# Fetching the cached rows of the sample stream one step early, into the buffers of the sample tokens

## The chip, the cores and the metric

The kernel runs on one core of one Trainium2 chip. The metric is the device time of one execution in microseconds (us); the number quoted for a kernel is the median of its timed runs.

## The reference, cut to what matters

The reference is one step of a one-layer encoder: a SwiGLU feed-forward block, an input projection with two groups of attention heads, and a second SwiGLU block. There are 1024 prompt tokens and 64 sample tokens; the sample tokens also attend to 1024 cached rows of keys and values.

```python
def macaron_half(x, g, b, w_gate, w_up, w_down):
    return layer_norm(ALPHA * x + 0.5 * swiglu(x, w_gate, w_up, w_down), g, b)

def mixer_sample(q_a, ..., pos, c_k_a, c_v_a, c_kidx, c_k_b, c_v_b, c_logf):
    ka_all = jnp.concatenate([c_k_a, k_a], axis=1)
    va_all = jnp.concatenate([c_v_a, v_a], axis=1)
    kb_all = jnp.concatenate([c_k_b, k_b], axis=1)
    vb_all = jnp.concatenate([c_v_b, v_b], axis=1)
    cum = jnp.cumsum(jnp.concatenate([c_logf, logf_b], axis=1), axis=1)
    ...
```

The cached rows are inputs: they depend on nothing that the kernel computes. The kernel needs them in another form, keys transposed, and every value split into a high and a low part (two float32r numbers whose sum is the float32 number). It makes that form while the first feed-forward block runs, and stores it in DRAM for the attention, which comes some hundreds of us later.

## The kernel before, in words

**The stage.** `ffn_a` (L203) computes gate and up products of a feed-forward block. It runs twice: L862 for the first block, with the cached work (`cgen`) as its argument `during`, and L1980 for the second, with an empty iterator. Otherwise both calls do the same work. It steps over j = 0 to 10, two slices of the hidden width each: `body0` (L258) for j = 0, and `body(j, u)` (L314) for j from 1, first for the gate weights (u = 0), then for the up weights (u = 1). Products follow a fast matrix-multiplication scheme with seven products of half-size blocks, each made of 12 matmuls (three for the split parts, by four).

**One body.** `raw_of` (L408, its DMA is L415) fetches two raw weight tiles of 128x1024, each by two DMAs. `split` (L107) copies a tile to its high part on ACT (L108) and makes the low part on DVE (L109). Four sums S1 to S4 of raw blocks are made on POOL (L327), then split on ACT (L330) and DVE (L331) to `Sh` and `Sl`. The products then go to PSUM and are evicted into a ring of 12 SBUF tiles (`ringz`): L340 on ACT, L342, L353, L355, L359, L361 on DVE, the gate's activation at L253 on ACT, gate times up at L256 on DVE. After u = 1, `emit_h` (L228) makes three sums on POOL (L231 to L234) and stores seven tiles (L236, to `hd0A` and `hd0S`). L353 of the next j writes a ring tile that one of these stores must have left. `emit_w` (L238) fetches two tiles of the down weights (L242), makes four sums (L245 to L248) and stores them (L250).

**The sample tokens.** The 64 sample rows ride along as matmuls `fs`. `sample(j)` (L372) evicts them to `sv` (L374, L375), makes `ssg` (L253, L256), and after the next body (`flush_late`, L390) transposes it on PE (L382) and stores it as `hs` (L384, L385).

**The buffers.** A tile is asked for by a tag; all tiles of a tag share so many buffers, and a DMA into a tile waits until an earlier tile of that tag is read for the last time. The tags that matter: `st` (3 buffers of 128x1024): the raw weights, and the cached rows `ckv` and `cka`; `wh` and `wl` (3 each): the split weights, and the split cached rows `chl`, `cha` and `cvt`; `hsh` (2 of 128x512): `ssg`, and the forget values `cf`; `hsl` (2 of 128x384): `hs`, and `lt`, `cm` of `cum_chunk`; `ssum` (4): `sv` and S1 to S4.

**The cached work.** `cached_all` (L841) is a generator; `ffn_a` calls `next(during)` four times per j (L311 in `body0`, L343 and L356 in `body`). Of each of the eight blocks of 128 cached rows (`cached_block`, L798) the first call fetches keys and values of group B into one `st` tile (L801, L802), transposes the keys by four PE transposes (L805, into the PSUM tile `ckb`), splits them to `chl` and stores both parts (L809); the second splits the values to `cvt` and stores them (L815); the third fetches group A's keys and values into another `st` tile (L818, L819), transposes (L821, into `cka`), splits to `cha`, and stores (L825, L828). Four last calls handle the forget values: a memset on POOL (L847), a fetch (L848), two transposes (L852, into `lfc`), a running sum on DVE (L836 to L838) and a store (L839). That is 28 calls, so it lasts to the end of j = 6.

**The order of the work.** All DMAs are issued from one queue, SP's. A scheduler orders each engine's instructions ahead of time, by their place in the program and by when it reckons that their inputs and buffers are there; on the chip each engine works through its list in order, and an instruction that waits holds up all behind it.

Of the kernel before, what the change touches and what calls it, by code (L numbers as in the profile page):

```python
# [9 lines left out]
F32 = mybir.dt.float32  # L10
F32R = mybir.dt.float32r
# [8 lines left out]
P = 128  # L20
# [9 lines left out]
HD = 64  # L30
# [17 lines left out]
def hybrid_step(ctx: ExitStack, tc: tile.TileContext, i, o):  # L48
    nc = tc.nc
    V, S, G, PE, DMA = nc.vector, nc.scalar, nc.gpsimd, nc.tensor, nc.sync  # L50
# [3 lines left out]
    ck_a = i["cache_k_a"].rearrange("l b s h d -> (l b s) h d")  # L54
    cv_a = i["cache_v_a"].rearrange("l b s h d -> (l b s) h d")
    ck_i = i["cache_kidx_a"].rearrange("l b s d -> (l b s) d")
    ck_b = i["cache_k_b"].rearrange("l b s h d -> (l b s) h d")
    cv_b = i["cache_v_b"].rearrange("l b s h d -> (l b s) h d")
    clf = i["cache_logf_b"].rearrange("l b s h -> (l b s) h")
# [9 lines left out]
    mp = ctx.enter_context(tc.tile_pool(name="mp", bufs=2, side="right"))  # L69
    sp = ctx.enter_context(tc.tile_pool(name="sp", bufs=4, side="right"))  # L70
    wp = ctx.enter_context(tc.tile_pool(name="wp", bufs=3, side="right"))
# [6 lines left out]
    def sm(name):  # L78
        return ps.tile([P, 512], F32, tag="sm", name=name, bufs=4)
# [7 lines left out]
    ident = cst.tile([P, P], F32, name="ident")  # L87
# [16 lines left out]
    def f(ap):  # L104
        return ap.bitcast(F32)

    def split(hi, lo, src):  # L107
        S.copy(hi, src)  # L108
        V.tensor_tensor(lo, src, f(hi), ALU.subtract)  # L109
# [645 lines left out]
    def load_x(xo, wg, wu):  # L755
# [12 lines left out]
        def put(t, hf):  # L768
# [11 lines left out]
    kacT = dp.tile([1, 2, P, PAST], F32, name="kacT")  # L780
    kbcT = dp.tile([4, 2, P, PAST], F32, name="kbcT")
    vaS, vbS, vacS, vbcS = (dp.tile([nh, P, 8, 2, HD], F32, name=nm)
                            for nm, nh in (("vaS", 2), ("vbS", 8), ("vacS", 2), ("vbcS", 8)))
    vaN, vbN = (dp.tile([DEC, nh, 2, HD], F32, name=nm) for nm, nh in (("vaN", 2), ("vbN", 8)))

    def v_rows(d, dn, t, h0, nh):
        return dn[:, h0:h0 + nh] if t == 8 else d[h0:h0 + nh, :, t].rearrange("h p s d -> p h s d")
    cumd_p = dp.tile([8, SEQ], F32, name="cumd_p")
    cumd_s = dp.tile([8, TT], F32, name="cumd_s")
# [5 lines left out]

    last_c = cst.tile([32, 1], F32, name="last_c")

    def cached_block(a):  # L798
        rs_ = slice(a * P, (a + 1) * P)
        kv = wp.tile([P, 1024], F32, tag="st", name="ckv")  # L800
        DMA.dma_start(kv[:, 0:512].rearrange("p (h d) -> p h d", h=8), ck_b[rs_])  # L801
        DMA.dma_start(kv[:, 512:1024].rearrange("p (h d) -> p h d", h=8), cv_b[rs_])  # L802
        pt = sm(f"ckb{a}")
        for q in range(4):
            PE.transpose(pt[:, q * P:(q + 1) * P], kv[:, q * P:(q + 1) * P], ident)  # L805
        hl = wp.tile([P, 1024], F32R, tag="wh", name="chl")
        split(hl[:, 0:512], hl[:, 512:1024], pt)
        for s in range(2):
            DMA.dma_start(kbcT[:, s, :, rs_].rearrange("a p t -> p a t"),  # L809
                          f(hl[:, s * 512:(s + 1) * 512]).rearrange("p (a t) -> p a t", a=4))  # L810
        yield
        vt = wp.tile([P, 1024], F32R, tag="wl", name="cvt").rearrange("p (h s d) -> p h s d", h=8, s=2)
        cv = kv[:, 512:1024].rearrange("p (h d) -> p h d", h=8)
        split(vt[:, :, 0, :], vt[:, :, 1, :], cv)
        DMA.dma_start(v_rows(vbcS, None, a, 0, 8), f(vt))  # L815
        yield
        kv = wp.tile([P, 1024], F32, tag="st", name="cka")
        DMA.dma_start(kv[:, 0:128].rearrange("p (h d) -> p h d", h=2), ck_a[rs_])  # L818
        DMA.dma_start(kv[:, 128:256].rearrange("p (h d) -> p h d", h=2), cv_a[rs_])  # L819
        pt = sm(f"cka{a}")  # L820
        PE.transpose(pt[:, 0:P], kv[:, 0:P], ident)  # L821
        hl = wp.tile([P, 1024], F32R, tag="wh", name="cha")
        split(hl[:, 0:P], hl[:, P:2 * P], pt[:, 0:P])
        for s in range(2):
            DMA.dma_start(kacT[0, s, :, rs_], f(hl[:, s * P:(s + 1) * P]))  # L825
        vt = hl[:, 512:768].rearrange("p (h s d) -> p h s d", h=2, s=2)
        split(vt[:, :, 0, :], vt[:, :, 1, :], kv[:, 128:256].rearrange("p (h d) -> p h d", h=2))
        DMA.dma_start(v_rows(vacS, None, a, 0, 2), f(vt))  # L828
        yield

    def cum_chunk(name, put_in, n, carry, dst):
        pt = sm(name)
        put_in(pt)
        lt = mp.tile([32, 384], F32, tag="hsl", name="lt")
        cm = mp.tile([32, 384], F32, tag="hsl", name="cm")
        V.tensor_copy(lt[:, :n], pt[:32, :n])  # L836
        V.tensor_tensor_scan(cm[:, :n], lt[:, :n], lt[:, :n], carry, ALU.add, ALU.bypass)
        V.tensor_copy(carry, cm[:, n - 1:n])  # L838
        DMA.dma_start(dst, cm[:8, :n])  # L839

    def cached_all():  # L841
        for a in range(8):
            yield from cached_block(a)
        V.memset(last_c, 0.0)
        for c in range(4):
            cf = mp.tile([P, 512], F32, tag="hsh", name="cf")[:, 0:64].rearrange("p (a h) -> p a h", a=2)
            G.memset(cf, 0.0)  # L847
            DMA.dma_start(cf[:, :, 0:8], clf[c * 256:(c + 1) * 256].rearrange("(a p) h -> p a h", p=P))  # L848

            def put_in(pt, cf=cf):  # L850
                for q in range(2):
                    PE.transpose(pt[:32, q * P:(q + 1) * P], cf[:, q, :], ident)  # L852

            cum_chunk(f"lfc{c}", put_in, 256, last_c, cumd_s[:, c * 256:(c + 1) * 256])
            yield

    cgen = cached_all()

    with tc.tile_pool(name="xe", bufs=1, side="left", reuse_waits="tile") as xe:
# [20 lines left out]
    for tl, bb in ((s0, (6, 7, 8)), (s1, (2, 3, 4, 5))):  # L880
        off = 0
        for b in bb:
            n = P * (b + 1) if b < 8 else TT
# [1016 lines left out]
    for fi, (jn, un) in enumerate(flat):  # L1900
# [22 lines left out]
        if len(pend) > AHEAD:  # L1923
            p, es = pend.pop(0)
# [114 lines left out]
```

## Time and profile before

| what | value |
|---|---|
| median of 3 runs | 2310.96 us (2305.94 to 2311.0) |
| the profiled execution, its own time | 2316.92 us |
| its span | 2315.1 us |
| PE busy | 95% of the span |
| DVE, ACT, POOL busy | 64%, 42%, 39% |
| DMA engines, mean share | 52% |

The profile gives the busy time of each engine (PE is TensorE's matmuls, PEld its weight loads, DVE VectorE, ACT ScalarE, POOL GpSimd, SP the engine that issues the DMAs). In a timeline each row has its start, its length, engine, line, operation, tile written and tile read; in square brackets stands how long the engine was idle before it, and what it then waited for. A row "A <- B" of a view of waits says that A waited for B: in total, how many times, and the longest.

### The profile page before, as it was taken

What the parts mean: (1) busy time and instruction counts of PE and PEld (TensorE: products, weight loads), DVE (VectorE), ACT (ScalarE), POOL (GpSimd) and SP (SyncE); (2) the same over time, 40 slices, a digit from 0 to 9 for tenths busy, and PEclk for the clock granted to TensorE, in tenths of its full rate; (3) what the DMA queues carried; (4) which work ended last, traced back from release to release, by engine and by line L of the source; (5) the groups of instructions that cost most, each with busy time, mean ns of one, the idle gap of its engine ahead of it and who ended that gap; (6) DMA issues with size and microseconds to landing.
All of it is one profiled execution on the core that took longest, in us unless ns stands there. A gap on an engine that the chain in (4) does not pass through costs nothing.

```text
span 2315.1 us, 33898 instructions
## 1 busy us (share of the span) xinstructions
PE 2207.0 (95%) x11832; PEld 1890.4 (82%) x11832; DVE 1490.7 (64%) x2359; ACT 965.1 (42%) x1776; POOL 902.5 (39%) x1058
## 2 busy tenths in 40 slices
PE   8999999999999999998899899997999999999997
PEld 7777878887888889997798778786888888877886
DVE  4556666556479746798567777676465565654677
ACT  4332332324344346732467777433233333333332
POOL 4545564641011323362434755113456465440011
PEclk9999999999999899999999999998999999999999
DMA  5656653448556344443757542564344344477554
GB/s 176 186 173 197 194 161 128 162 166 299 188 181 205 119 118 125 140 127 109 204 146 206 147 118 68 174 213 132 106 155 154 124 161 143 138 253 248 174 182 154
DMA packets 330837, 379.31 MB, mean 164 GB/s; under 512 B 43556, under 2 KB 226276, under 8 KB 330664
## 3 DMA queue, kind: packets, MB, share of 16 engines
q1 hardware_dynamic: 330664, 377.13, 51.7%
q8 instruction: 94, 1.54, 0.3%
q14 instruction: 79, 0.65, 0.1%
HBM read 256.51 MB, written 120.53 MB: 163 GB/s over the span
## 4 chain that ended last, share of the span: by engine, by line
PE 43%; DVE 5%; DMA 3%; issue 1%; POOL 1%; ACT 1%; SPq 0%; DVEq 0%; ACTq 0%; POOLq 0%
PE fa L114 9%; PE fbP L114 8%; PE fz L114 5%; PE fy L114 3%; PE gb L114 3%; PE pq L114 3%; PE acc L114 2%; PE pt L1706 2%; PE fs L114 2%; PE ip L114 1%; PE fbs L114 1%; PE sq L114 1%; PE gb_a L114 1%; PE gb_b L114 1%; PE sacc L114 0%
## 5 line engine op out<-in xcount | busy, mean ns | idle before, releaser
L114 PE MATMUL fbP<-ml,lh 128*128 128x512 f32 x616 | 238.6, 391 | 1.8 <-DVE ml L109 1.8
L114 PE MATMUL fbP<-mh,ll 128*128 128x512 f32 x616 | 237.9, 390 | 2.1 <-DVE ll L109 2.1
L108 ACT CAST wh<-wst 128x1024 fp32r<-128x1024 f32 x108 | 113.7, 1054 | 292.6 <-PE fs L114 114.0
L114 PE MATMUL fbP<-mh,lh 128*128 128x512 f32 x616 | 223.5, 391 | 2.7 <-ACT lh L108 1.7
L109 DVE TENSOR_TENSOR wl<-wst,wh 128x1024 fp32r<-128x1024 f32 x108 | 158.2, 1466 | 77.2 <-ACT wh L108 69.0
L108 ACT CAST lh<-raw 128x1024 fp32r<-128x1024 f32 x84 | 82.5, 982 | 228.1 <-PE fbP L114 194.7
L331 DVE TENSOR_TENSOR Sl<-S,Sh 128x512 fp32r<-128x512 f32 x160 | 162.7, 1025 | 23.0 <-ACT Sh L330 22.5
L109 DVE TENSOR_TENSOR ll<-raw,lh 128x1024 fp32r<-128x1024 f32 x84 | 100.0, 1191 | 115.4 <-ACT lh L108 115.0
L327 POOL TENSOR_TENSOR S<-wst 128x512 f32<-128x512 f32 x80 | 122.2, 1527 | 133.2 <-DMA wst<-ffn_w_gate 47.6
L662 POOL TENSOR_TENSOR zz<-u,zz 128x512 f32<-128x512 f32 x16 | 25.6, 1613 | 378.6 <-DVE u L684 267.7
L330 ACT CAST Sh<-S 128x512 fp32r<-128x512 f32 x160 | 97.0, 620 | 173.7 <-PE fa L114 96.6
L327 POOL TENSOR_TENSOR S<-wst,S 128x512 f32<-128x512 f32 x40 | 65.8, 1645 | 220.8 <-issue 218.7
L114 PEld LDWEIGHTS fbP<-ml,lh 128*128 128x128 f32 x616 | 115.5, 188 | 27.9 <-DVE ml L109 4.4
L114 PEld LDWEIGHTS fbP<-mh,lh 128*128 128x128 f32 x616 | 115.2, 188 | 28.1 <-ACT mh L108 2.4
L114 PEld LDWEIGHTS fbP<-mh,ll 128*128 128x128 f32 x616 | 115.7, 188 | 26.8 <-DVE ll L109 3.0
L1643 POOL TENSOR_SCALAR e<-e,su 128x128 f32<-128x128 f32 (+7 forms) x128 | 97.0, 770 | 90.1 <-DVE su L1640 68.6
L114 PE MATMUL acc<-pp,vs 128*128 128x256 f32 (+1 forms) x640 | 116.0, 304 | 4.6 <-DVE pp L109 3.0
L109 DVE TENSOR_TENSOR pp<-pt,pp 128x512 fp32r<-128x512 f32 (+1 forms) x160 | 99.0, 632 | 32.6 <-ACT pp L108 31.4
L114 PE MATMUL ip<-iwh,xh 128*128 128x256 f32 (+3 forms) x384 | 115.9, 302 | 1.7 <-ACT o L1019 0.8
L114 PE MATMUL ip<-iwl,xh 128*128 128x256 f32 (+3 forms) x384 | 112.8, 294 | 0.0
L114 PE MATMUL ip<-iwh,xl 128*128 128x256 f32 (+3 forms) x384 | 112.8, 294 | 0.0
L353 DVE TENSOR_TENSOR ringz<-fz,ringz 128x512 f32<-128x512 f32 x40 | 27.6, 690 | 119.5 <-DMA hd0S<-ringz 44.2
(505 smaller groups left out, 6836.0 us busy)
## 6 DMA issues: line engine op xcount, KB each, us to landing
wst<-ffn_w_gate SPq DMA_DIRECT2D x88, 256.0 KB
wst<-ffn_w_up SPq DMA_DIRECT2D x88, 256.0 KB
w<-ffn_w_down SPq DMA_DIRECT2D x44, 512.0 KB
raw<-ffn_w_down SPq DMA_DIRECT2D x40, 512.0 KB
wst<-w_out SPq DMA_DIRECT2D x24, 512.0 KB
hd0T<-w SPq DMA_DIRECT2D x44, 256.0 KB
hd0S<-ringz SPq DMA_DIRECT2D x44, 256.0 KB
hd1T<-w SPq DMA_DIRECT2D x44, 256.0 KB
```

The lines of the kernel that those rows point to most:

```text
L108: S.copy(hi, src)
L109: V.tensor_tensor(lo, src, f(hi), ALU.subtract)
L114: last_mm[:] = [PE.matmul(out, lhsT, rhs, start=start, stop=stop, skip_group_check=more).ins]
L327: G.tensor_tensor(t, ss[0] if x is None else x, ss[1] if y is None else y, op)
L330: S.copy(hi, t)
L331: V.tensor_tensor(lo, t, f(hi), ALU.subtract)
L353: V.tensor_tensor(c22, Z, c12, ALU.add)
L662: eng.tensor_tensor(z_of(t, d), acc, z_of(t, d), ALU.add)
L1643: G.tensor_scalar(es[q][:, :n], es[q][:, :n], su2[:, q:q + 1], 1.0, ALU.mult, ALU.mult)
L1706: PE.transpose(pt[:, m * P:(m + 1) * P], e[:, kt * P:(kt + 1) * P], ident)
```

## The change

The cached work is cut into steps of two parts, a fetch and a use, and each call does the fetch of one step and then the use of the step before it. The raw rows move from the tag `st` to the tags `hsh` (keys of B, values of B, each a tile of its own) and `hsl` (keys and values of A together). The forget values are cut in the same way. The instructions and the bytes moved are the same; there is one call more (29).

```diff
-    def cached_block(a):
-        kv = wp.tile([P, 1024], F32, tag="st", name="ckv")
-        DMA.dma_start(kv[:, 0:512].rearrange("p (h d) -> p h d", h=8), ck_b[rs_])
-        DMA.dma_start(kv[:, 512:1024].rearrange("p (h d) -> p h d", h=8), cv_b[rs_])
...
-        kv = wp.tile([P, 1024], F32, tag="st", name="cka")
...
+    def cached_steps():
+        for a in range(8):
+            def fetch(parts, tag):
+                w = sum(x.shape[1] for x in parts) * HD
+                kv = mp.tile([P, 512 if tag == "hsh" else 384], F32, tag=tag, name="craw")
+                c = 0
+                for x in parts:
+                    n = x.shape[1]
+                    DMA.dma_start(kv[:, c:c + n * HD].rearrange("p (h d) -> p h d", h=n), x[rs_])
+                    c += n * HD
+                return kv
...
+            yield lambda: fetch((ck_b,), "hsh"), keys_b
+            yield lambda: fetch((cv_b,), "hsh"), values_b
+            yield lambda: fetch((ck_a, cv_a), "hsl"), both_a
+        for c in range(4):
+            def fetch_f(c=c):
+                if c == 0:
+                    V.memset(last_c, 0.0)
+                cf = mp.tile([P, 512], F32, tag="hsh", name="cf")[:, 0:64].rearrange("p (a h) -> p a h", a=2)
+                G.memset(cf, 0.0)
+                DMA.dma_start(cf[:, :, 0:8], clf[c * 256:(c + 1) * 256].rearrange("(a p) h -> p a h", p=P))
+                return cf
...
+            yield fetch_f, sums_f
     def cached_all():
-        for a in range(8):
-            yield from cached_block(a)
...
+        use = None
+        for fetch, nxt in cached_steps():
+            raw = fetch()
+            if use is not None:
+                use[0](use[1])
             yield
+            use = nxt, raw
+        use[0](use[1])
+        yield
```

`keys_b`, `values_b` and `both_a` hold the transposes, splits and stores of the three old calls, unchanged; `sums_f` holds the transposes and the running sum.

## Rows read from the trace of the kernel before

**Rows 1.** The page: busy time of the engines, share of the span, instructions.
```profile
PE 2207.0 (95%) x11832; PEld 1890.4 (82%) x11832; DVE 1490.7 (64%) x2359; ACT 965.1 (42%) x1776; POOL 902.5 (39%) x1058
```

**Rows 2.** Windows: stretch, length, busy per engine (instructions), PE clock, DMA share, GB/s.
```profile
53.41:527.85 474.44, 459.01 (x2155) 379.76 (x2154) 272.81 (x326) 147.72 (x243) 250.80 (x168) 0.98 0.54 171
1616.45:2060.45 444.00, 444.00 (x2107) 371.96 (x2106) 248.61 (x282) 136.47 (x211) 235.10 (x160) 1.00 0.43 143
```

**Rows 3.** PE's timeline, 60 to 515 (instructions after idle time), and its waits, 0 to 600.
```profile
78.81 0.80 PE L114 MATMUL fa<-B11h,wh 128*128 128x512 f32 x1 [2.39 <-ACT wh L108]
80.28 0.80 PE L114 MATMUL fy<-T2h,Sh 128*128 128x512 f32 x1 [0.24 <-ACT Sh L330]
82.54 0.79 PE L114 MATMUL fa<-B11h,wl 128*128 128x512 f32 x1 [1.03 <-DVE wl L109]
100.78 0.50 PE L114 MATMUL fa<-T1h,Sh 128*128 128x512 f32 x1 [1.50 <-ACT ringz L253]
...
327.27 0.38 PE L852 MATMUL lfc<-ident,cf 128*32 128x128 f32 x2 [1.36 <-DMA cf<-cache_logf_b]
332.20 0.79 PE L114 MATMUL fz<-T4h,wh 128*128 128x512 f32 x1 [3.12 <-DVE ringz L353]
```
```profile
PE fz L114 <- DVE ringz L353: 6.3, 3, 3.1
...
PE fa L114 <- DVE ringz L355: 2.5, 2, 1.3
```

**Rows 4.** Windows of 40 us, columns as in rows 2.
```profile
20.00:60.00 40.00, 40.00 (x234) 34.76 (x233) 18.19 (x26) 17.51 (x32) 23.63 (x18) 1.00 0.35 115
...
60.00:100.00 40.00, 35.61 (x147) 27.77 (x145) 20.09 (x22) 10.96 (x20) 15.43 (x10) 0.87 0.59 177
300.00:340.00 40.00, 35.51 (x159) 29.14 (x158) 24.00 (x31) 11.40 (x17) 26.20 (x19) 0.91 0.52 169
```

**Rows 5.** Timeline of SP, 58 to 73: the gate weights of j = 1.
```profile
70.53 0.37 SPq L415 DMA_DIRECT2D wst<-ffn_w_gate  x1
```

**Rows 6.** Waits of the SP queue, 60 to 360.
```profile
SPq L415 <- PE cka L821: 15.5, 4, 6.1
```

**Rows 7.** Timeline of SP in the second feed-forward block, 1570 to 1575.
```profile
1571.88 2.02 SPq L415 DMA_DIRECT2D wst<-ffn_w_gate  x4
```

**Rows 8.** Timeline of ACT, 56 to 104.
```profile
99.18 1.05 ACT L108 CAST wh<-wst 128x1024 fp32r<-128x1024 f32 x1 [8.79 <-DMA wst<-ffn_w_up]
```

**Rows 9.** Waits by engine, 60 to 360: POOL, DVE, ACT.
```profile
POOL S L327 <- DMA wst<-ffn_w_gate: 47.6, 5, 14.5
```
```profile
DVE ringz L353 <- DMA hd0S<-ringz: 28.3, 3, 10.5
```
```profile
ACT wh L108 <- DMA kbcT<-chl: 16.9, 5, 5.1
```

**Rows 10.** Timelines of SP and DVE, 130 to 150.
```profile
136.56 0.97 SPq L242 DMA_DIRECT2D w<-ffn_w_down  x2
137.63 1.87 SPq L236 DMA_DIRECT2D hd0S<-ringz  x3
```
```profile
146.90 0.69 DVE L353 TENSOR_TENSOR ringz<-fz,ringz 128x512 f32<-128x512 f32 x1 [10.54 <-DMA hd0S<-ringz]
```

**Rows 11.** Timelines of SP and ACT, 125 to 142: one fetch and the first use.
```profile
125.43 0.37 SPq L801 DMA_DIRECT2D ckv<-cache_k_b  x1
```
```profile
141.09 0.59 ACT L108 CAST chl<-ckb 128x512 fp32r<-128x512 f32 x1 [0.29 <-PE ckb L805]
```

**Rows 12.** Timelines of POOL and ACT, 120 to 133.
```profile
126.29 1.36 POOL L327 TENSOR_TENSOR S<-wst,S 128x512 f32<-128x512 f32 x1 [10.01 <-issue]
```
```profile
131.25 0.62 ACT L330 CAST Sh<-S 128x512 fp32r<-128x512 f32 x1 [3.08 <-PE fa L114]
```

**Rows 13.** Timeline of POOL, 300 to 345: the first and the last memset of `cf`.
```profile
304.15 0.14 POOL L847 MEMSET cf<- 128x64 f32 x1
...
341.36 0.15 POOL L847 MEMSET cf<- 128x64 f32 x1 [11.45 <-PE hs L382]
```

More of the change, by code (lines that the diff above doesn't have):

```diff
@@ L796, in hybrid_step @@
     last_c = cst.tile([32, 1], F32, name="last_c")
-    def cached_block(a):
-        rs_ = slice(a * P, (a + 1) * P)
-        kv = wp.tile([P, 1024], F32, tag="st", name="ckv")
-        DMA.dma_start(kv[:, 0:512].rearrange("p (h d) -> p h d", h=8), ck_b[rs_])
-        DMA.dma_start(kv[:, 512:1024].rearrange("p (h d) -> p h d", h=8), cv_b[rs_])
[L803 to L816, printed above, removed]
-        kv = wp.tile([P, 1024], F32, tag="st", name="cka")
[L818 to L829, printed above, removed]
@@ new lines, in cached_steps, with keys_b, values_b, both_a @@
+    def cached_steps():
+        for a in range(8):
+            rs_ = slice(a * P, (a + 1) * P)
+            def fetch(parts, tag):
[7 more added lines that the diff above has]
+                return kv
+            def keys_b(kv, a=a, rs_=rs_):
+                pt = sm(f"ckb{a}")
+                for q in range(4):
+                    PE.transpose(pt[:, q * P:(q + 1) * P], kv[:, q * P:(q + 1) * P], ident)
+                hl = wp.tile([P, 1024], F32R, tag="wh", name="chl")
+                split(hl[:, 0:512], hl[:, 512:1024], pt)
+                for s in range(2):
+                    DMA.dma_start(kbcT[:, s, :, rs_].rearrange("a p t -> p a t"),
+                                  f(hl[:, s * 512:(s + 1) * 512]).rearrange("p (a t) -> p a t", a=4))
+            def values_b(kv, a=a):
+                vt = wp.tile([P, 1024], F32R, tag="wl", name="cvt").rearrange("p (h s d) -> p h s d", h=8, s=2)
+                split(vt[:, :, 0, :], vt[:, :, 1, :], kv.rearrange("p (h d) -> p h d", h=8))
+                DMA.dma_start(v_rows(vbcS, None, a, 0, 8), f(vt))
+            def both_a(kv, a=a, rs_=rs_):
+                pt = sm(f"cka{a}")
+                PE.transpose(pt[:, 0:P], kv[:, 0:P], ident)
+                hl = wp.tile([P, 1024], F32R, tag="wh", name="cha")
+                split(hl[:, 0:P], hl[:, P:2 * P], pt[:, 0:P])
+                for s in range(2):
+                    DMA.dma_start(kacT[0, s, :, rs_], f(hl[:, s * P:(s + 1) * P]))
+                vt = hl[:, 512:768].rearrange("p (h s d) -> p h s d", h=2, s=2)
+                split(vt[:, :, 0, :], vt[:, :, 1, :], kv[:, 128:256].rearrange("p (h d) -> p h d", h=2))
+                DMA.dma_start(v_rows(vacS, None, a, 0, 2), f(vt))
+            yield lambda: fetch((ck_b,), "hsh"), keys_b
[9 more added lines that the diff above has]
+                return cf
+            def sums_f(cf, c=c):
+                def put_in(pt):
+                    for q in range(2):
+                        PE.transpose(pt[:32, q * P:(q + 1) * P], cf[:, q, :], ident)
+                cum_chunk(f"lfc{c}", put_in, 256, last_c, cumd_s[:, c * 256:(c + 1) * 256])
+            yield fetch_f, sums_f
@@ L841, in cached_all @@
     def cached_all():
-        for a in range(8):
-            yield from cached_block(a)
[L844 to L854, printed above, removed]
+        use = None
[3 more added lines that the diff above has]
+                use[0](use[1])
             yield
+            use = nxt, raw
+        use[0](use[1])
+        yield
     cgen = cached_all()
```

## The prediction

> **What bounds the kernel now.** I read first the busy shares: PE is at work 95% of the span [rows 1], so only what lets PE work more closely can shorten the kernel. Next, the stage that the change touches. The kernel holds its own control: `ffn_a` runs a second time without cached work. Windows from the first product behind j = 0's `fs` to the last `fs` show 474.44 us for the first run against 444.00 us for the second [rows 2]. The 30.44 us more consist of three things. PE is idle for 474.44 - 459.01 = 15.43 us, against none in the second run. It runs 48 instructions more (2155 against 2107), which are the cached transposes. And its clock is 0.98 against 1.00 in the mean.
>
> Then the timeline and the waits of PE, for each idle time [rows 3]. There are ten, together 15.3 us: a cluster of three around 80, one at 100.78, five between 147 and 333 that end with an eviction on DVE (6.3 + 2.5 us), and one at 327.27. After the cluster (2.39 + 0.24 + 1.03 us) a stretch runs at half clock (1.2 instead of 2.4 GHz): the window's granted clock is 0.87, so 40 x 0.13 = 5.2 us of work are lost [rows 4]. After the 3.12 us at 332.20 the window shows 0.91, or 3.6 us [rows 4]; the other gaps cost no clock. Idle time and clock together are 15.3 + 5.2 + 3.6 = 24.1 us; the remaining 6.3 us, some 0.13 us for each of 48 transposes, stay. So 24.1 us, 1.0% of the span, is all that the cached rows cost beyond their own matmuls, and the most that the change can give back here.
>
> Last, the waits behind those gaps. The gate weights of j = 1 come in two `st` tiles: the second is asked for only at 70.53 [rows 5], though j = 0 has long split its own. In the second run all four DMAs go out within 2.02 us at 1571.88 [rows 7], and no gap follows. The SP queue tells why: the fetch of weights waits 15.5 us in four places for the transpose of `cka`, which holds an `st` tile [rows 6]. POOL waits 47.6 us in five places for gate weights [rows 9].
>
> **The change, part by part.** It removes no instruction and no byte; PE's own work is the same. It moves the raw rows from 16 tiles of `st` to 24 smaller ones of `hsh` and `hsl`, and fetches them one step earlier.
>
> *The `st` tiles.* The cluster at 78.81 goes: the weights can be asked for when j = 0 has split its last tile, as in the second run, where none of the three gaps exists. That is 3.66 us idle and 5.2 us of clock, 8.9 us. The gap of 1.50 us at 100.78 has the same root: ACT's copy of the up weights waits 8.79 us for their DMA [rows 8], and the activation that PE needs stands behind that copy. It goes too: 1.5 us.
>
> *The evictions.* Five gaps end with DVE's L353 or L355, 8.8 us, of which 3.12 us stand at 332.20 with their 3.6 us of clock behind them. L353 waits 28.3 us in three places for a store of the step before [rows 9]. Part of that is late weights, which hold up POOL's sums and, through the queue of SP, the stores. Part is not: at 137.63 the store goes out right behind two fetches of down weights and L353 is released only at 146.90 [rows 10], and ACT's copy of the weights waits 16.9 us in five places for `kbcT`, a store from a `wh` tile that the change leaves where it is [rows 9]. Bounds: 0 and 8.8 + 3.6 = 12.4 us. The rows lie on both sides, so I take half, 6.2 us.
>
> *One step ahead.* The forget values' gap of 1.36 us at 327.27 is PE waiting for a fetch, which will now have a whole call's time: 1.4 us. For the keys the earlier fetch hides nothing more: a fetch goes out at 125.43 and its transposes are copied at 141.09 [rows 11], 15.7 us later, and no gap of PE ends with a cached fetch of keys.
>
> *The new users of `hsh`.* Program order gives its two buffers to keys, values, `ssg` and `cf` in turn. In calls 5, 14 and 26 the new tile finds `ssg` in one buffer and the tile of the step before in the other, so it waits for that step's transposes: in these three the fetch isn't early, and what SP or POOL has behind it waits. Behind it stand weights, now far ahead of need, and `emit_h`'s stores. The trace of before has one such wait, POOL's last memset, held 11.45 us by `hs` [rows 13]; it cost PE nothing. I bound the new waits by 0 and that 11.4 us, and take one gap like the 3.12 us [rows 3]: 3 us, since three fetches are affected and weights are early.
>
> *SP and the start.* The fetches keep their queue and number. At the start they can go out a little earlier, as nothing holds `hsh`; PE has no idle time from 20 to 60 us [rows 4], so 0.64 MB earlier (one block's rows) is covered by products; if that cover fails, it costs up to 3.7 us (0.64 MB at the stage's 171 GB/s [rows 2]).
>
> Sum: 8.9 + 1.5 + 6.2 + 1.4 - 3 = 15.0 us. The profiled execution would go from 2316.92 to 2301.9; it stands 6.0 us above the median of the runs, 2310.96, from which 15.0 us leave **2296.0 us**. A measurement can tell 0.3%, 6.9 us.
>
> A rule bears on the evictions. The Trainium skill (DMA: Bandwidth & Descriptors, section "Queues, rings and completion order") says that each DMA engine consumes the descriptors of one issuing queue in ring order. The wait of rows 10 agrees with it, the two fetches being ahead of the store. By it, a cached fetch issued sooner is one more transfer ahead of such a store.
>
> **The rivals.** (a) *All gaps go*, as in the second run: 24.1 us, 2286.9 us. For it: the second run has the same evictions and stores and no gap. Against it: the DMA share of 0.54 against 0.43 [rows 2] and the `wh` tiles stay.
>
> (b) *The stores stay late.* Their landing is set by the bytes in front, which are the same, and the eviction gaps stay in full: 8.9 + 1.5 + 1.4 - 3 = 8.8 us, 2302.2 us. The order rule of the Trainium skill stands on this side.
>
> (c) *The change doesn't do what it says*: the weights arrive early but their copies wait for `wh`, of which `chl` and `cha` hold one until they are stored [rows 9], and the first gap moves there. Only the gaps of 1.5 and 1.4 us go: 2.9 us, 2308.1 us. Against it: the longest wait of the stage is POOL's of 14.5 us for gate weights, the longest for a store of `chl` 5.1 us [rows 9].
>
> (d) *Slower: the sample tokens wait for `hsh`.* While a raw tile holds each buffer, `ssg` can't be written, `sv` keeps its `ssum` buffer and S4 of the next body is late. The sum waits for that buffer already: it idles 10.01 us and starts at 126.29, ends at 127.65, and ACT takes it at 131.25 [rows 12], a margin of 3.6 us. A raw tile can hold its buffer 15.7 us [rows 11], so one sample can cost PE up to 12 us. Three of seven samples that are so late cost 36 us, and against the 18 us won elsewhere leave 18 us more: 2329 us. It decides from (18 + 6.9) / 7 = 3.6 us lost per sample, a delay of 7.2 us each. Against it: buffers seem to be handed out in program order (the first `cf` is set only at 304.15 [rows 13], though its tag had a free buffer much earlier), so a later fetch can't overtake `ssg`, and in each j one buffer is read before `ssg` comes.
>
> **How the numbers follow.** Forecast 0.42, (a) 0.12, (b) 0.16, (c) 0.18, (d) 0.12. Faster by over 0.3%: the forecast, (a) and (b), 0.70; within 0.3%: (c), 0.18; slower: (d), 0.12. The range runs from (a)'s time, 2286, to 2311, which takes in (c) and the case in which new waits take the whole 11.4 us while the evictions keep their gaps (2310.6); it leaves out (d) and some of the spread, under 0.2.
>
> **What would show it.** Right: in the timeline of PE no idle time at the start of j = 1 and full clock there; all gate weights of j = 1 on SP before 50 us; no SP wait of weights for `cka`; POOL's 47.6 us of waits for gate weights mostly gone; the stage some 459 us long instead of 474. Wrong on the evictions: gaps ending with L353 as many as now. (c) would show as PE waiting for ACT's `wh` behind `kbcT`, (d) as POOL's fourth sum waiting for `ssg` and PE for `Sh`. The forecast is wrong if the stage isn't at least 7 us shorter, or if PE idles anywhere after 540 us by some us more than now.

## The result and the profile after

The changed kernel takes 2288.57 us (median of five runs, 2287.26 to 2291.06), beside 2311.0 us of the kernel before in the same comparison: a ratio of 0.9902, 95% interval 0.9887 to 0.9918, or 22.4 us less. The prediction of 2296.0 us named the sign and its range holds the time; the gain is 7.4 us larger than its sum of 15.0, and 1.7 us below rival (a)'s 24.1. The profiled execution is the one of 2291.06 us. Ratios compare runs at the usual granted clock; two runs of all, at 0.65 and 0.74, took far longer and are left out of them.

The busy shares and the windows of the kernel after, which answer to [rows 1, 2, 4]. The first window runs from the first product behind j = 0's `fs` to the last `fs` of the first feed-forward stage.

```profile
PE 2193.7 (96%) x11832; PEld 1883.3 (82%) x11832; DVE 1497.6 (65%) x2359; ACT 963.1 (42%) x1776; POOL 901.3 (39%) x1058
```
```profile
54.50:507.30 452.80, 450.97 (x2155) 375.76 (x2154) 276.49 (x326) 148.27 (x243) 250.66 (x168) 1.00 0.55 176
60.00:100.00 40.00, 38.99 (x184) 32.21 (x183) 23.68 (x27) 13.44 (x24) 26.79 (x18) 1.00 0.63 198
300.00:340.00 40.00, 40.00 (x195) 33.14 (x194) 30.03 (x36) 14.07 (x21) 24.58 (x18) 1.00 0.43 133
```

PE has the same 2155 instructions in the stage, which is 474.44 - 452.80 = 21.6 us shorter. Idle time fell from 15.4 us to 452.80 - 450.97 = 1.8 us, which is 13.6 us; PE's busy time fell by 459.01 - 450.97 = 8.0 us, and as the work is the same this is mainly clock: the granted clock is 1.00 in the stage and in both windows that had 0.87 and 0.91. The stage begins 1.1 us later than before (54.50 against 53.41). So it ends 20.5 us sooner, about what the medians differ by. From one profiled execution to the other the span shrinks by some 5 us more behind the stage, where the code is the same; the medians do not bear those out, and they are not claimed here.

The waits of PE in the stage, where [rows 3] had ten gaps:

```profile
PE fy L114 <- ACT Sh L330: 1.0, 1, 1.0
PE fz L114 <- DVE ringz L353: 0.8, 2, 0.5
```

The SP queue from 20 to 34 us. It answers to [rows 5], where the last gate weights of j = 1 were asked for at 70.53:

```profile
21.70 1.04 SPq L415 DMA_DIRECT2D wst<-ffn_w_gate  x2
...
27.29 0.93 SPq L415 DMA_DIRECT2D wst<-ffn_w_gate  x2
```

The fetch of weights no longer waits for a transpose: the line of [rows 6] is gone from SP's waits. The waits of POOL, DVE and ACT from 20 to 350 us answer to [rows 9]:

```profile
POOL S L327 <- DMA wst<-ffn_w_gate: 6.4, 1, 6.4
```
```profile
DVE ringz L353 <- DMA hd0S<-ringz: 11.5, 4, 4.7
```
```profile
ACT wh L108 <- DMA kbcT<-chl: 14.2, 5, 5.0
ACT wh L108 <- DMA kacT<-cha: 13.0, 3, 6.6
```

POOL's 47.6 us behind gate weights are 6.4 now, and DVE's 28.3 us behind the stores of the step before are 11.5 (14.9 in the window of [rows 9], 60 to 360 us), the longest 4.7 instead of 10.5. ACT's waits for the stores that free a `wh` tile stay; those for `kacT` rose from 5.5 to 13.0 us. None of them ends a gap of PE by itself, but the gap of 0.37 us at 142.06 goes back to one of 5.67 us for `kacT`.

### The profile page after: what moved, and what is told of

It reads as the page before. It is cut to its first block, busy times and chain, and to the rows that moved or that the text cites. A ratio compares the mean times of both kernels' runs of the same rounds, so it can differ in the third digit from the quotient of the medians.

```text
span 2289.3 us, 33886 instructions
## 1 busy us (share of the span) xinstructions
PE 2193.7 (96%) x11832; PEld 1883.3 (82%) x11832; DVE 1497.6 (65%) x2359; ACT 963.1 (42%) x1776; POOL 901.3 (39%) x1058
## 4 chain that ended last, share of the span: by engine, by line
PE 45%; DVE 4%; DMA 2%; issue 1%; ACT 1%; POOL 1%; SPq 0%; DVEq 0%; ACTq 0%; POOLq 0%
PE fa L114 10%; PE fbP L114 8%; PE fz L114 5%; PE fy L114 3%; PE pq L114 3%; PE gb L114 3%; PE acc L114 3%; PE pt L1730 2%; PE fs L114 2%; PE ip L114 2%; PE fbs L114 1%; PE gb_a L114 1%; PE sq L114 1%; PE gb_b L114 1%; DVE pp L109 1%
## 5 line engine op out<-in xcount | busy, mean ns | idle before, releaser
L327 POOL TENSOR_TENSOR S<-wst 128x512 f32<-128x512 f32 x80 | 122.6, 1532 | 110.1 <-DVE Sl L331 50.4
L114 PEld LDWEIGHTS fbP<-mh,lh 128*128 128x128 f32 x616 | 115.5, 188 | 27.8 <-ACT lh L108 2.0
L109 DVE TENSOR_TENSOR ml<-raw,mh 128x1024 fp32r<-128x1024 f32 x84 | 101.4, 1211 | 2.1 <-ACT mh L108 2.0
```

The source lines that it names most:

```text
L114: last_mm[:] = [PE.matmul(out, lhsT, rhs, start=start, stop=stop, skip_group_check=more).ins]
L327: G.tensor_tensor(t, ss[0] if x is None else x, ss[1] if y is None else y, op)
```

## The experiments

The change does two things, and the first pair of runs parts them. All ratios are to runs of the kernel before on the same chip (medians 2309.9 to 2311.7 us). "The stage" is the window of [rows 2], cut at the same two instructions.

**Raw rows in `hsh` and `hsl`, but not ahead.** From the kernel after:

```diff
-        use = None
...
-            raw = fetch()
-            if use is not None:
-                use[0](use[1])
+            nxt(fetch())
...
-            use = nxt, raw
-        use[0](use[1])
-        yield
```

> The raw rows stand in the tags hsh and hsl as in the changed kernel, but each is fetched in the call that uses it, as before. Theory S (what paid is that no cached row holds an st tile any more): 2286 to 2294 us, the stage from the first fy to the last fs some 453 us long, at most the forget values' gap of 1.4 us back. Rival A (what paid is the fetch one step early): 2304 to 2312 us, with gaps of PE that end with transposes or copies of cached rows.

Measured: 2290.35 us, 0.9915 [0.989, 0.9941]. Its stage, and the one gap of PE above 0.2 us in it:

```profile
53.20:506.60 453.40, 451.10 (x2156) 375.96 (x2155) 276.05 (x326) 149.07 (x244) 246.76 (x168) 1.00 0.55 176
```
```profile
312.26 0.38 PE L854 MATMUL lfc<-ident,cf 128*32 128x128 f32 x2 [2.08 <-DMA cf<-cache_logf_b]
```

Without any fetch ahead the stage is within 0.6 us of the changed kernel's. What is lacking is the forget values' wait, back with 2.08 us. With the new tiles the gain does not need the earlier fetch.

**Ahead, but in `st`.** From the kernel after, keys and values of B in one `st` tile as before, those of A in another:

```diff
-                kv = mp.tile([P, 512 if tag == "hsh" else 384], F32, tag=tag, name="craw")
+                kv = wp.tile([P, 1024], F32, tag="st", name="craw")
...
-            yield lambda: fetch((ck_b,), "hsh"), keys_b
-            yield lambda: fetch((cv_b,), "hsh"), values_b
...
+            yield fetch_b, keys_b
+            yield lambda: kv_b[0][:, 512:1024], values_b
```

> The fetch one step early, but the raw rows of groups A and B in st tiles as before (a tile for keys and values of B, one for A). Theory S: no gain, 2306 to 2325 us, since an st tile is now held longer; PE's gap at the start of j = 1 and the gaps that end with L353 are there, and half clock with them. Rival A: 2286 to 2296 us.

Measured: 2296.83 us, 0.9944 [0.9927, 0.996]: 14 us gained, where theory S expected nothing; rival A's range is missed by 0.8 us. The stage, and two of the five gaps of PE between 77 and 90 us (5.3 us together):

```profile
53.60:517.80 464.20, 455.98 (x2156) 377.80 (x2155) 274.04 (x326) 147.18 (x244) 255.68 (x168) 0.99 0.55 175
```
```profile
77.45 0.50 PE L114 MATMUL fa<-B11h,wh 128*128 128x512 f32 x1 [1.30 <-ACT wh L108]
...
83.64 0.50 PE L114 MATMUL fa<-B21h,wh 128*128 128x512 f32 x1 [2.31 <-ACT ringz L340]
```

The cluster at the start of j = 1 is still there, as it must be if two raw tiles in `st` at that time are its cause. But of the gaps that end with an eviction on DVE (L353 or L355) 0.2 us are left, though the raw rows are in `st`. So theory S has half of it. Two differences from the kernel before are left that can do it: the earlier fetch, and that every transpose and split comes one call later. The next two runs do one of them each.

**One call later, nothing else.** From the kernel before, one empty step ahead of the first:

```diff
+        yield
         for a in range(8):
```

> The kernel before, whose cached work starts one call later: raw rows in st, fetched in the call that uses them. The uses fall in the same calls as in e2, the fetches don't come early. Theory P (in e2 it was the place of the uses among the products, not the early fetch, that took away the gaps at the evictions): 2292 to 2301 us. Theory E (the early fetch did it): 2306 to 2316 us.

Measured: 2295.65 us, 0.992 [0.9897, 0.9942]. By the medians one `yield` gives 16 of the 22 us. In the profiled executions the stage is 8.5 us shorter and begins 1.4 us sooner; the other 6 us are not accounted for. The stage:

```profile
52.00:517.90 465.90, 455.55 (x2156) 377.86 (x2155) 270.02 (x326) 147.67 (x244) 248.90 (x168) 0.99 0.55 174
```

Between 54 and 110 us two gaps of 1.1 and 1.0 us stand where the cluster was. The second fetch of B's rows now goes out at 74.5 instead of 27.8, so up to there only one raw tile stands in `st` while j = 1 asks for its weights; the gap of 1.0 us is PE waiting for that late fetch. The evictions still cost 7.0 us (before 8.8), which theory P did not foresee.

**Ahead in `st`, each use in its old call.** From the second experiment: the first call fetches two steps.

```diff
             if use is not None:
                 use[0](use[1])
-            yield
+                yield
```

> Raw rows in st, fetched one step early, with the uses in the same calls as in the kernel before (the first call fetches two steps). Theory P: 2304 to 2316 us, with gaps of PE that end with L353 or L355. Theory E: 2291 to 2300 us, few such gaps.

Measured: 2304.9 us (eight runs), 0.9972 [0.9953, 0.9991]: the early fetch alone gives some 6.5 us. The forget values' gap is still there, with 1.7 us. The stage and the two longest gaps of the start:

```profile
50.40:520.20 469.80, 457.20 (x2156) 379.33 (x2156) 278.84 (x326) 147.91 (x244) 258.72 (x168) 0.99 0.54 172
```
```profile
75.83 0.50 PE L114 MATMUL fa<-B11h,wh 128*128 128x512 f32 x1 [2.35 <-ACT wh L108]
...
96.82 0.80 PE L114 MATMUL fa<-B11h,wh 128*128 128x512 f32 x1 [3.04 <-ACT wh L108]
```

By the medians the place of the uses is worth more (16 us against 6.5), as theory P said. But its reason fails: of the 8.8 us of eviction gaps the place alone leaves 7.0 and the early fetch alone 3.5, nearly all of that one gap of 3.13 us at 325.31; only both together leave 0.2. Much of what the place wins lies at the start, where it leaves one raw tile in `st` instead of two.

**Four calls later.** From the kernel before:

```diff
+        for _ in range(4):
+            yield
         for a in range(8):
```

> The kernel before, whose cached work starts four calls later, after all of j = 0. Theory S2: the cluster at the start of j = 1 and its half clock go (8.9 us), since no cached row stands in st there; gaps at the evictions are left, their number depending on the place: 2294 to 2306 us. If the start of j = 1 has its gaps as before, S2 falls there.

Measured: 2295.29 us, 0.9927 [0.9904, 0.9951]; the stage is 459.80 us. No gap from 54 to 110 us, at full clock, and eviction gaps of 5.1 us further on. One raw tile does stand in `st` at the start, against what was expected: B's first fetch goes out at 29.0, and the tile is read until 67 us. It gives no more than the shift by one: away from the start of j = 1, raw rows in `st` go on costing evictions here.

**A's rows alone out of `st`; B's rows alone.** From the kernel before, each fetched in its own call:

```diff
-        kv = wp.tile([P, 1024], F32, tag="st", name="cka")
+        kv = mp.tile([P, 384], F32, tag="hsl", name="cka")
```
```diff
-        kv = wp.tile([P, 1024], F32, tag="st", name="ckv")
+        kv = mp.tile([P, 512], F32, tag="hsh", name="ckv")
...
-        cv = kv[:, 512:1024].rearrange("p (h d) -> p h d", h=8)
+        cv = mp.tile([P, 512], F32, tag="hsh", name="ccv").rearrange("p (h d) -> p h d", h=8)
```

> The kernel before, with only the raw rows of group A (cka) moved from st to hsl, fetched in the call that uses them. Theory S2 (the harm is that weights must wait for an st tile that a cached row holds, worst where two are held at once, as ckv and cka at the start of j = 1): no wait of weights for cka is left, and one cached row at a time stays in st: 2286 to 2298 us, PE idle in the first stage 0 to 8 us instead of 15.4. Rival D (keys and values of B, held longest, do the harm): 2303 to 2312 us.

> The kernel before, with only the raw rows of group B moved from st to hsh (keys and values a tile each, each fetched in the call that uses it); cka stays in st. Theory S2: the long holds go, the wait of weights for the transpose of cka stays: 2290 to 2304 us, with PE idle 3 to 10 us in the first stage. Rival D: 2286 to 2292 us.

Measured: A alone 2291.98 us, 0.9915 [0.9892, 0.9938], 19 us less; B alone 2289.49 us, 0.9901 [0.9881, 0.9921], 22 us less. Each alone gives about what both give, so the parts do not add: the larger part of the cost arises when two raw tiles stand in `st` at once. Neither has the cluster at the start of j = 1; B alone has three gaps, 1.6 us together, from 109 to 112 us. B alone came out 0.5 us below theory S2's range and within rival D's, but A alone, at 11 us below D's range, rules D out. The stage of each, and the longest gap of each, an eviction:

```profile
53.10:511.40 458.30, 453.36 (x2156) 377.25 (x2155) 271.75 (x326) 147.97 (x244) 245.15 (x168) 1.00 0.55 175
```
```profile
190.54 0.76 PE L114 MATMUL fz<-T4h,wh 128*128 128x512 f32 x1 [3.27 <-DVE ringz L353]
```
```profile
50.90:507.70 456.80, 452.82 (x2156) 377.19 (x2155) 273.98 (x326) 148.61 (x244) 246.86 (x168) 1.00 0.55 176
```
```profile
319.18 0.80 PE L114 MATMUL fz<-T4h,wh 128*128 128x512 f32 x1 [2.37 <-DVE ringz L353]
```

**One `st` tile taken away.** The reverse test: raw rows as in the kernel after, but one more `st` tile is allocated ahead of a feed-forward stage, written once, and read behind it into a tile that nobody uses. First in each of the two stages with a copy as the reading instruction (here the second stage):

```diff
+    held = wp.tile([P, 1024], F32, tag="st", name="held")
+    V.memset(held[:, 0:1], 0.0)
...
+    V.tensor_copy(sink, held[:, 0:1])
```

> The changed kernel; one of the three st tiles is held by an unused tile during the second run of the feed-forward stage, which has no cached work. Theory S with its second part (late weights alone also make the evictions at L353 late, by POOL's and SP's order): the second stage goes from 444 to 452 to 470 us, with gaps at L353 or L355 among those of PE, total 2296 to 2315 us. Rival B (the evictions' gaps came from the cached rows' own stores): only gaps that end with weights (wh, wl, Sh), none with L353 or L355. Rival C (two tiles are enough): 2286 to 2293 us.

> The changed kernel; one of the three st tiles is held by an unused tile during the first run of the stage. Theory S: most of the gain is lost, 2302 to 2325 us, the first stage 465 to 490 us long instead of 453. Rival A: 2286 to 2294 us.

Measured: 2286.84 us, 0.9893 [0.9871, 0.9915], and 2285.99 us, 0.9889 [0.9862, 0.9915]. Neither held anything. The copy depends on nothing in the stage and ran ahead of it; its line in the kernel for the first stage, at 0.9 us:

```profile
L890 DVE COPY sink<-held x1: 154/154/154, 0.9 to 0.9; 128x1 f32<-128x1 f32 x1
```

They say nothing on the question and serve as two more measurements of the changed kernel. Then with an addition that also reads the last ring tile of the stage, so that it can't run sooner (again the second stage):

```diff
+    V.memset(held[:, 0:512], 0.0)
...
+    V.tensor_tensor(sink, xo2[0].ring[(xo2[0].at - 1) % 12], held[:, 0:512], ALU.add)
```

> The changed kernel, with one st tile held through the whole second run of the stage (its release depends on the last tile of the stage). Weights have two tiles, which one body needs both. Theory S2 with the second part (late weights alone make the evictions at L353 late): the second stage goes from 444 to 448 to 465 us, and gaps at L353 or L355 are among those of PE; total 2291 to 2310 us. Rival B (the evictions' gaps came from the cached rows' stores): gaps end only with weights and their sums (wh, wl, Sh). Rival C (two tiles are enough, only two held at once hurt): 2284 to 2291 us, no gap.

> The changed kernel, with one st tile held through the whole first run of the stage. Theory S2: between 2291 and 2315 us, the first stage 456 to 480 us instead of 453, since the cached rows' splits and stores come on top. Rival C: 2284 to 2291 us.

Measured, second stage: 2287.53 us, 0.9892 [0.9872, 0.9912]. The addition ran at 2044.6 us, behind the stage, which takes what it took before [rows 2], against the second part of theory S2:

```profile
1585.90:2030.20 444.30, 444.16 (x2107) 371.84 (x2106) 241.89 (x281) 135.23 (x211) 251.96 (x160) 1.00 0.44 143
```

First stage: 2298.2 us, 0.9949 [0.993, 0.9969], some 10 us above the changed kernel. The stage, its longest gap, and two waits from 60 to 360 us:

```profile
51.90:512.70 460.80, 452.72 (x2156) 376.84 (x2155) 270.55 (x326) 147.69 (x244) 250.75 (x168) 1.00 0.55 173
```
```profile
322.98 0.80 PE L114 MATMUL fz<-T4h,wh 128*128 128x512 f32 x1 [3.28 <-DVE ringz L353]
```
```profile
POOL S L327 <- DMA wst<-ffn_w_up: 36.7, 6, 9.0
```
```profile
DVE ringz L353 <- DMA hd0S<-ringz: 25.3, 5, 7.8
```

Two `st` tiles suffice for the weights where no cached work runs beside them. Beside it they don't: POOL waits 36.7 us for up weights (8.2 in the changed kernel), DVE's wait for stores is back at 25.3 us (14.9), and three eviction gaps (7.0 us) return, with no raw row in `st`. So late weights and cached work together make those gaps, and the waits for stores rise with the late weights.

**Rows in their own call, forget values ahead.** Built from what the first experiment left over: keys, values and A's rows as there, only the forget values one step early. From the kernel after:

```diff
-        for fetch, nxt in cached_steps():
-            raw = fetch()
-            if use is not None:
-                use[0](use[1])
+        steps = cached_steps()
+        for _ in range(23):
+            fetch, nxt = next(steps)
+            nxt(fetch())
...
+        for c in range(4):
+            after = next(steps, None)
+            ahead = after[0]() if after else None
+            nxt(raw)
+            raw, nxt = ahead, after and after[1]
+            yield
```

> As e1 (raw rows in hsh and hsl, fetched in the call that uses them), but the forget values fetched one step early. Theory S2: the gap of 2.1 us before the forget values' transposes in e1 goes and no other comes: under 1 us of idle time of PE in the first stage, 2285 to 2290 us, the same as the changed kernel within what can be measured. Against it: more than 2 us idle there, or a time above 2292 us.

Measured: 2288.53 us (six runs), 0.9911 [0.9893, 0.9929], equal to the changed kernel's 2288.57. In the trace its stage is the closest to the floor, 444.0 us and 6.3 us of transposes:

```profile
54.70:505.60 450.90, 450.71 (x2156) 376.29 (x2156) 273.67 (x326) 148.94 (x244) 246.47 (x168) 1.00 0.56 177
```

All kernels side by side. Evictions are the idle time of PE in the stage that ends with L353 or L355; the start is its idle time from 60 to 110 us. Up to 2.7 us of idle time in a stage is neither, and half clock is in neither column.

| kernel | raw tiles in `st` while j = 1 asks for weights (30 to 75 us) | start, us | evictions, us | stage, us | median, us |
|---|---|---|---|---|---|
| before | two | 5.2 | 8.8 | 474.4 | 2311.0 |
| ahead in `st`, old calls | two | 7.0 | 3.5 | 469.8 | 2304.9 |
| ahead in `st` | two | 5.3 | 0.2 | 464.2 | 2296.8 |
| one call later | one | 2.0 | 7.0 | 465.9 | 2295.7 |
| four calls later | one, until 67 us | 0 | 5.1 | 459.8 | 2295.3 |
| A alone out | one | 0 | 4.9 | 458.3 | 2292.0 |
| B alone out | one | 0.3 | 2.4 | 456.8 | 2289.5 |
| after, one tile held | one, the held one | 1.0 | 7.0 | 460.8 | 2298.2 |
| same call | none | 0 | 0 | 453.4 | 2290.4 |
| after | none | 1.0 | 0.8 | 452.8 | 2288.6 |
| forget values ahead | none | 0 | 0 | 450.9 | 2288.5 |

## Why the prediction was right, and where its sum was short

**The start of j = 1 (8.9 + 1.5 us): right.** The cluster and the gap at 100.78 are gone and the window from 60 to 100 us has full clock; one gap of 1.0 us has come in. The root is shown as well: the cluster stands in the three kernels that hold two raw tiles in `st` at that time and in none that holds one or none.

**The evictions (6.2 of 12.4 us): the step that failed.** 0.8 us of gaps are left and no half clock, so by the prediction's count some 11.6 us went. The prediction halved the term because part of DVE's wait for stores "is not" late weights, and because the `wh` tiles stay. The `wh` waits did stay (14.2 us for `kbcT`, before 16.9) and cost PE no more than 0.4 us. The store waits did not: from 60 to 360 us they fell from 28.3 to 14.9 us with the same stores and the same fetches in the same queue, to 3.0 us with each fetch in its own call, and rose to 25.3 us when one `st` tile was taken away. The second run of the stage, whose store waits the prediction did not read, shows what is normal. From 1616 to 2060 us of the kernel before, without cached work and without a gap of PE, DVE waits for stores as well:

```profile
DVE ringz L353 <- DMA hd1S<-ringz: 27.2, 7, 4.6
```

So a store wait of up to 4.6 us is there in any case and costs nothing. The long ones, 8.7 to 10.5 us, went with the late weights and came back with them (7.8 us with one tile held): they are a result of them, not a second cause. One eviction gap of the kernel before, 1.74 us at 197.54, has no store wait in front of it and does go back to a `wh` wait. ACT's copy waits for `kbcT`, DVE's split behind it for the copy, and L353, at 196.81, stands behind DVE's splits:

```profile
190.65 1.05 ACT L108 CAST wh<-wst 128x1024 fp32r<-128x1024 f32 x1 [5.07 <-DMA kbcT<-chl]
```
```profile
191.73 1.23 DVE L109 TENSOR_TENSOR wl<-wst,wh 128x1024 fp32r<-128x1024 f32 x1 [5.40 <-ACT wh L108]
```

In the changed kernel the same chain behind a wait of 5.67 us for `kacT` leaves a gap of 0.37 us, at 142.06, and a `kbcT` wait of 5.04 us leaves none. So the `wh` tiles were a second cause, worth at least 1.7 us before and 0.4 us after, where the prediction kept half of 12.4 us for them and the stores. The rule of the Trainium skill that stood on rival (b)'s side (DMA: Bandwidth & Descriptors, section "Queues, rings and completion order") is neither borne out nor refuted: no run changed the ring order alone, and behind the waits that are left PE has one gap of 0.45 us.

**The clock (5.2 + 3.6 us): counted too high.** The prediction takes the loss of a whole window as lost work, but in part of the half clock PE was idle, and that time is in the 15.3 us already. These are the first stretch of half clock and the second from the end of its gap on:

```profile
78.40:88.64 10.24, 8.55 (x20) 5.84 (x21) 10.24 (x8) 4.64 (x9) 10.16 (x6) 0.50 0.61 193
332.20:337.81 5.61, 5.61 (x14) 4.45 (x15) 3.69 (x7) 1.57 (x2) 0.00 (x0) 0.50 0.10 28
```

Half of 8.55 and of 5.61 us is 4.3 + 2.8 = 7.1 us lost, so the bound of 24.1 us is 22.4. That this equals the measured gain is partly luck, as 1.8 us of gaps are left and PE's busy time fell by 8.0 us.

**The new users of `hsh` (-3 us): mis-sized, 0.** In the whole stage SP waited 1.3 us for a transpose to free a raw tile, POOL's sum 1.2 us for `ssg`, and POOL's memset of `cf` 6.5 us for the forget values' transpose. None ends a gap of PE. The one new gap, 1.0 us for `Sh` at 78, is not theirs: with 1.1 us it also stands in the kernel that is only one call later, which has no raw row in `hsh`.

**One step ahead (1.4 us): right in the trace.** The forget values' gap is gone; with the fetch back in its call it is 2.1 us. In the medians that is 1.8 us (2290.4 against 2288.6), less than can be told apart. The gap does not hang on the fetch ahead alone: it is absent in three kernels without one (one call later, A alone, B alone) and stands in one that has it (ahead in `st`, old calls). That the keys' earlier fetch hides nothing was right too: with it and without it the kernel takes 2288.6 and 2288.5 us.

**SP and the start (0): within 1.1 us.** The stage begins between 50.4 and 54.7 us in these kernels, and latest in one that fetches no rows ahead; the earlier fetch does not set it.

The evictions and `hsh` make 5.4 + 3 us, against 7.4 us that the median fell short; the new gap of 1.0 us is about the difference. The clock counted too high works the other way and is not in this sum. **Rival (a)** described the trace best, with a chance of 0.12: its control, the second run of the stage, was the stronger evidence, and the DMA share set against it does not decide, for it is 0.55 in the changed kernel. **(b)** fell with the eviction gaps, **(c)** with the `wh` waits that cost 0.4 us, **(d)** with the 1.2 us for `ssg`; the wait of 10.01 us that (d) starts from names no buffer in its row ([rows 12] has `issue`).

**Open.** Why the place of the uses and the time of the fetch change the eviction gaps so much (0.2 to 8.8 us) while raw rows are in `st`. Time with two tiles held does not order the kernels: from SP's fetch to the last read of each raw tile it is some 96 us in all before, 46 us one call later, and 136 us ahead in `st`, which has the fewest eviction gaps of the three. Nor does the wait of the weights for `cka` on SP, 15.5 us before [rows 6] and 14.8 us ahead in `st`. The steps fall between other products then, but which ones decide was not tried. Every edit also gives the scheduler another order to work with, and no run holds that order fixed.

## What to carry to other kernels

A ring shared by quick and slow users is as short as its slowest user makes it at the worst moment: count the tiles held at once there, and compare with the same stage run without the extra work, which gave the gain to within 2 us here. Here moving either one of two competing users out gave nearly the whole gain, so it is worth trying the cheaper move first. Before a prefetch is credited with a gain, run the kernel with the prefetch undone and the uses left in place, and with the uses moved by one empty step: here the fetch ahead was worth some 2 us with the rows out of `st` and 6.5 us with them in it, and the empty step 16 us. An instruction that is to hold a buffer must read something that the stage makes last, or it runs ahead of it.

## What the runs showed that was not expected

Gaps of nearly the same length cost different amounts of clock. Before, 3.12 us at 332.20 were followed by half clock up to 337.81, which is 2.8 us of lost work (the second of the two rows under **The clock**, above). With one tile held, 3.28 us at 322.98 were followed by half clock only up to 326.24, or 1.6 us:

```profile
322.98:326.24 3.26, 3.26 (x8) 2.61 (x9) 3.15 (x6) 1.57 (x2) 1.23 (x1) 0.50 0.03 3
```

In that kernel a gap of 2.35 us at 234.52 cost no clock (first row), while with B alone out the gap of 2.37 us at 319.18 did, 40 x 0.04 = 1.6 us (second row):

```profile
220.00:260.00 40.00, 37.66 (x178) 31.04 (x177) 28.44 (x33) 12.73 (x23) 21.09 (x15) 1.00 0.60 185
```
```profile
300.00:340.00 40.00, 37.63 (x178) 30.96 (x177) 27.73 (x34) 12.46 (x20) 23.26 (x18) 0.96 0.36 114
```

So the clock behind a gap has to be read from its window, not from the gap's length, and only where PE is at work in it.
